# Three edits to a two-block fp32 network on one core: where tiles start, which PSUM banks GLA's scores use, how a layer norm gets its statistics

## The chip, the cores and the metric

The kernel runs on one core of one Trainium2 chip. TensorE multiplies matrices out of SBUF into PSUM, VectorE, ScalarE and GpSimd work on vectors, SyncE issues most DMAs. The metric is the device time of one execution in microseconds (us); smaller is better. The profile comes from one profiled execution.

## The reference

The input is a sequence of 256 rows of width 1024. A first block adds a hybrid mixer (three kinds of attention, gated and merged) and a convolutional FFN, both with RMS norms that are modulated by a vector. The second block has two layers: a gated linear attention (GLA, 4 heads of 128 keys and 256 values) and a dilated sliding-window attention (SWA), each followed by a layer norm. The part that the change touches:

```python
def layer_norm(x, g, b):
    mu = jnp.mean(x32, axis=-1, keepdims=True)
    xc = x32 - mu
    var = jnp.mean(xc * xc, axis=-1, keepdims=True)
    return (xc * lax.rsqrt(var + LN_EPS) * g + b)
...
def second_block(x, ...):
    for layer in range(DEPTH_2):
        y = gla_mixer(...) if layer == 0 else dilated_mixer(...)
        x = layer_norm(DEEPNORM_ALPHA * x + y, ln_g[layer], ln_b[layer])
...
# in gla_mixer: o = q S with a state S that decays by exp(log_a) at every row and key:
att = jnp.einsum('bhid,bhjd,bhijd->bhij', qc, kc, decay)
```

All weights, activations and results are float32.

## The kernel before

**Products in three parts.** An fp32 product is made of three fp32r matmuls: every operand is split into a high half and the rest, a low half, and `mm3` adds low stationary by high moving, high by low, and high by high in one PSUM bank. Weights are streamed by `Stream`: `_chunk` (L147 on) issues a DMA into `raw`, ScalarE copies it to `whi` (L158) and VectorE subtracts to get `wlo` (L159). Activations have tiles that end in `hi` and `lo` (`hhi`, `hlo`, `mhi`, `mlo`, `h2`, `x2`, `x3`, `fhi`/`flo`, `ohi`/`olo`, `shi`/`slo`).

**Two kinds of product.** In `wstat` (keys in1, inc, zg, br, up, gla, gk, kvk, sq) a 128x128 block of weights stands in TensorE and 256 columns of activations move. In `tokmm` (keys out, dn, gvg, gout, kvv, sout) 128 rows of the sequence stand and 512 columns of weights move. `wpair` can run a pair "fresh": first all high-activation products of eight blocks, then all low ones.

**Where tiles start.** `PAST` is 48 elements, 192 bytes: every low tile is allocated a little wider and used from 192 bytes past its start, whichever operand it is. The eight-block activations come from `big8`, with one tag for high tiles and one for low.

**GLA's scores.** The decayed scores of a half batch of 128 rows are built by levels. `gla_x` makes, for each of four heads, a bank `pm` with two matmuls (names glamr, Ll, Lh), its exponential E on ScalarE (L1024) and the products Xk, Xq on VectorE (L1027, L1028). `gla_p` then makes for each level four 128x64 matmuls (names Xq, Xk) into a bank, and VectorE copies from it under a mask into attT (COPY_PREDICATED, L1044, L1050). PSUM banks come from three rotating tags: `acc` (4), `mm` (2), `at` (2). `pm` and the score banks are all `at`. A scheduler with priorities puts these in between the products of GLA's v and g weights (names whi, wlo, x2hi, x2lo into acc); each engine then runs its instructions in that order.

**GLA's layer norm.** `layer_norm` walks a list of steps, `ORD3` for this one and `ORD4` for the last one. A step has a letter, a batch half (b = 0 or 1) and a column half. u: u = alpha x + y with a running sum; c: mean from the sums, then ScalarE's square of 1024 columns with a running sum (`junk`); w: (u − mean) times the gain; r: `rstd`, VectorE's add (`ms`) and GpSimd's power (`rs`, L364); n: scaling on ScalarE, N: on VectorE. TensorE then transposes the result x (L891), and the products of SWA need those transposes. A `Queue` keeps the steps of an engine in the written order. Helpers record many operations under line L193, so names tell them apart.

Of the kernel before, what the change touches and what calls it, by code (L numbers as in the profile page):

```python
# [8 lines left out]
F32 = mybir.dt.float32  # L9
F32R = mybir.dt.float32r  # L10
# [8 lines left out]
S = 256  # L19
# [8 lines left out]
SIDE = [("inc", 0)] + [("zg", i) for i in range(10)] + [("out", 0)] + [("up", i) for i in (3, 7, 11, 15)]  # L28
ORD1 = "s00 m01 s01 m00 r0 a00 S00 a01 S01 m10 s10 R0 A00 A01 s11 r1 m11 n00 n01 a10 S10 a11 S11 A10 R1 A11 N10 n11"
ORD2 = "s00 m01 s01 m00 r0 a00 a01 s10 m10 s11 r1 m11 a10 a11"  # L30
ORD3 = "u00 u01 c0 w00 w01 r0 n00 n01 u10 u11 c1 w10 w11 r1 N10 N11"
ORD4 = "u00 u01 c0 w00 w01 r0 u10 o00 u11 c1 o01 w10 r1 w11 o10 o11"
SC_SWA = float(128.0 ** -0.5)


PAST = 48

COLS = {}
# [64 lines left out]
class Stream:  # L103
# [31 lines left out]
    def _chunk(self, i):  # L135
        nc = self.nc
        key, ap, n, part = self.items[i]
        if part < 0:
            raw = self.early.tile([128, n], F32, tag="early", name="early", bufs=3)
        else:  # L140
            raw = self._raw()
        if not part:
            for o in range(0, n, 1024):
                nc.sync.dma_start(raw[:, o:o + 1024], ap[:, o:o + 1024])
            self.done.append(raw)
            return
        nc.sync.dma_start(raw[:, :n], ap)  # L147
        parts = []
        for o in range(0, n, part) if part > 0 else range(0, -part, 1024):
            m = min(part, n - o) if part > 0 else min(1024, -part - o)  # L150
            hi = self.pool.tile([128, 1024], F32R, tag="whi", name="whi", bufs=self.hlbufs)
            lo = self.pool.tile([128, 1088], F32R, tag="wlo", name="wlo", bufs=self.hlbufs)
            lo = lo[:, PAST:PAST + 1024]
            with ExitStack() as st:
                for ins in self.behind:
                    st.enter_context(self.tc.issue_after(ins))
                st.enter_context(self.tc.high_priority(self.pri))
                i0 = nc.scalar.activation(hi[:, :m], raw[:, o:o + m], AF.Copy)  # L158
                i1 = nc.vector.tensor_sub(lo[:, :m], raw[:, o:o + m], hi[:, :m].bitcast(F32))  # L159
                self.last = (i0.ins, i1.ins)  # L160
            parts.append((hi, lo))
        self.done.append((part, parts) if part > 0 else (raw, (1024, parts)))
# [68 lines left out]
def hybrid_blocks(ctx, tc, A, out, dbg=None):  # L231
# [22 lines left out]
    def at_t():  # L254
        return ps.tile([128, 512], F32, tag="at", name="at", bufs=2)
# [139 lines left out]
            mm(pr[:, 256 + b:257 + b], ssq[:, b * 128:(b + 1) * 128], ones[:, 0:1], h == 0 and b == 0, h == 3, True)  # L395

    def big8(dt, name, past=0):
        t = cn.tile([128, KK * S + 64 * (past > 0)], dt, name=name, tag="big8l" if past else "big8h")
        return t[:, past:past + KK * S].rearrange("p (k s) -> p k s", k=KK)

    hT = (big8(F32R, "hhi"), big8(F32R, "hlo", PAST))
# [375 lines left out]
    for i in range(2):  # L777
# [12 lines left out]
            branch2(0)  # L790
            branch2(1)
        gates(9 + 2 * i)
    mT = (big8(F32R, "mhi"), big8(F32R, "mlo", PAST))
    for i in range(4):
        if i > 1:
            branch2(i)
# [138 lines left out]
    def ffn_up(f):  # L935
        p = wpair(("up", f), h2, f == 0)
        u = wk.tile([128, S], F32, name="u", tag="u", bufs=2)
        cw = lambda i: col("cw", i * NF + f)
        act.activation(u, p[:, 0:S], AF.Identity, scale=cw(2), bias=col("cb", f))
        dve.scalar_tensor_tensor(u[:, 1:S], p[:, 0:S - 1], cw(1), u[:, 1:S], op0=OP.mult, op1=OP.add)  # L940
        dve.scalar_tensor_tensor(u[:, 2:S], p[:, 0:S - 2], cw(0), u[:, 2:S], op0=OP.mult, op1=OP.add)
        act.activation(u, u, AF.Gelu_apprx_tanh)
        a = wk.tile([128, S], F32, name="fa", tag="fa", bufs=2)
        dve.tensor_mul(a, u, p[:, S:2 * S])
        hi = wk.tile([128, 1, S], F32R, name="fhi", tag="fhi", bufs=6)
        lo = wk.tile([128, 1, S + 64], F32R, name="flo", tag="flo", bufs=6)[:, :, PAST:PAST + S]
        ins = act.activation(hi[:, 0, :], a, AF.Copy)
        ins2 = dve.tensor_sub(lo[:, 0, :], a, hi[:, 0, :].bitcast(F32))
        fact[f] = (hi, lo)
        return ins, ins2  # L950
# [13 lines left out]
    x2 = res.tile([128, 2, D], F32, name="x2")  # L964
    rms_residual(y2, x1, mod[3], x2, ORD2)
    dump("x2", x2)
    x2T = (big8(F32R, "x2hi"), big8(F32R, "x2lo", PAST))
    ws.behind = transposes(x2, ev_split(x2T), last_mm)


# [41 lines left out]
    def gla_x(b, u):  # L1012

        Xk = p3.tile([128, 4, 4, 128], F32, name="Xk", tag="Xk", bufs=1)
        Xq = p3.tile([128, 4, 4, 128], F32, name="Xq", tag="Xq", bufs=1)
        XK[b, u] = (Xk, Xq)
        nk, nq = (4, 4) if u == 0 else (3, 3) if b == 0 else (3, 4)
        for h in range(4):
            pm = at_t()
            r = glam[:, 4 * u * (1 + b):4 * u * (1 + b) + 4, :]  # L1020
            mm(pm, Ll[:, b, h * 128:(h + 1) * 128], r, True, False)
            mm(pm, Lh[:, b, h * 128:(h + 1) * 128], r, False, True)
            E = p3.tile([128, 4, 128], F32, name="E", tag="E", bufs=2)
            act.activation(E, pm, AF.Exp, scale=1.0 / 16.0)  # L1024
            bs = slice(b * 128, (b + 1) * 128)
            bc = lambda x, n: x[:, h, bs][:, None, :].to_broadcast([128, n, 128])
            dve.tensor_mul(Xk[:, h, 0:nk, :], E[:, 0:nk, :], bc(kT, nk))  # L1027
            dve.tensor_mul(Xq[:, h, 0:nq, :], E[:, 0:nq, :], bc(qT, nq))  # L1028
            if u and b == 0:
                dve.tensor_mul(keep[:, h, :], E[:, 3, :], kT[:, h, bs])  # L1030
            if h % 2:
                yield

    def gla_p(b, u):

        Xk, Xq = XK[b, u]
        for l in range(4):
            pp = at_t()
            if 4 * u + l < 7:
                n = 64 >> (4 * u + l)  # L1040
                late = lambda x: x.rearrange("p (g t s) -> p g t s", t=2, s=n)[:, :, 1, :]
                for h in range(4):
                    mm(pp[:, h * 64:(h + 1) * 64].rearrange("p (g s) -> p g s", s=n), Xk[:, h, l, :], late(Xq[:, h, l, :]), True, True)
                dve.copy_predicated(attT[:, 2 * b].rearrange("p h (g t s) -> p h g t s", t=2, s=n)[:, :, :, 1, :],  # L1044
                                    late(glamask[:, 4 * u + l, :])[:, None].to_broadcast([128, 4, 64 // n, n]),
                                    pp[:, 0:256].rearrange("p (h g s) -> p h g s", h=4, s=n))
                continue
            for h in range(4):
                mm(pp[:, h * 128:(h + 1) * 128], kT[:, h, b * 128:(b + 1) * 128], qT[:, h, b * 128:(b + 1) * 128], True, True)
            dve.copy_predicated(attT[:, 2 * b], glamask[:, 4 * u + l, :][:, None, :].to_broadcast([128, 4, 128]),  # L1050
                                pp.rearrange("p (h q) -> p h q", h=4))
        if u and b:
            pp = at_t()
            for h in range(4):
# [51 lines left out]
    for i in range(2, 4):  # L1106
        w = ws.get(("gvg", 4 + i), 1)
        work += [(x2T, 2 * i + u, w, u * 1024) for u in range(2)]
    gla_out(0)
    oT = (p3.tile([128, KK, S], F32R, name="ohi", tag="Xk"),  # L1110
          p3.tile([128, KK * S + 64], F32R, name="olo", tag="Xq")[:, PAST:PAST + KK * S].rearrange("p (k s) -> p k s", k=KK))
    pe = Queue(tc, pe, ws.last[0])

    def gated(b, u, last):
# [43 lines left out]
    def layer_norm(x, y, grow, brow, dst, utile, order, after=None):  # L1158


        qa, qd = Queue(tc, act, ws.last[0]), Queue(tc, dve, ws.last[1])
        su, r, u, w = {}, {}, {}, {}
        with tc.high_priority(BOOST):
            for step in order.split():
                op, b, h = step[0], int(step[1]), int(step[2:] or 0)
                c = half(h)
                if op == "u":
                    if not h:
                        su[b] = cn.tile([128, 6], F32, name="su", tag="su", bufs=2)
                        u[b], w[b] = utile(b), utile(b + 2)  # L1170
                    qd.scalar_tensor_tensor(u[b][:, c], x[:, b, c], ALPHA, y[b][h], op0=OP.mult, op1=OP.add, accum_out=su[b][:, h:h + 1])
                elif op == "c":
                    qd.tensor_scalar(su[b][:, 2:3], su[b][:, 0:1], su[b][:, 1:2], -1.0 / (32.0 * D), op0=OP.add, op1=OP.mult)
                    qd.tensor_scalar(su[b][:, 3:4], su[b][:, 2:3], -32.0, None, op0=OP.mult)
                    qa.activation(junk(), u[b], AF.Square, bias=su[b][:, 2:3], scale=1.0 / 32.0, accum_out=su[b][:, 4:5])
                elif op == "w":
                    qd.scalar_tensor_tensor(w[b][:, c], u[b][:, c], su[b][:, 3:4], grow[:, c], op0=OP.subtract, op1=OP.mult)
                elif op == "r":
                    r[b] = rstd(su[b][:, 4:5], 1, 1e-5, qd)
                elif op == "n":  # L1180
                    qa.activation(dst[:, b, c], w[b][:, c], AF.Copy, scale=r[b][:, 0:1])
                elif op == "N":
# [106 lines left out]
    def swa_pv(i, parts=(slice(0, S),)):  # L1289
# [1 line left out]
        kv, pT = i // 2, pTs[i]  # L1291
        v = lambda g, b: sl(sv, ALL, b, slice((2 * g + kv) * 128, (2 * g + kv + 1) * 128))
        hi = wk.tile([128, 2, S], F32R, name="shi", tag="shi", bufs=2)
        lo = wk.tile([128, 2 * S + 64], F32R, name="slo", tag="slo", bufs=2)[:, PAST:PAST + 2 * S].rearrange("p (u s) -> p u s", u=2)
        for u in range(2):
            sact[2 * i + u] = sl((hi, lo), ALL, slice(u, u + 1))
        for qs in parts:
# [148 lines left out]
```

## Time and profile before

| what | value |
|---|---|
| median of 3 runs | 735.49 us (733.15 to 735.66) |
| profiled execution, its own time | 735.57 us |
| its span, first to last instruction | 733.6 us |
| mean granted TensorE clock | 0.987 |
| instructions | 12191 |

The span is what the trace covers; some 2 us lie around it. In the trace, PE is TensorE's matmuls and PEld its weight loads, DVE is VectorE, ACT ScalarE, POOL GpSimd. A matmul's shown length overlaps that of the next, so its cost is taken from start to start. `[1.22 <-ACT E L1024]` behind a row means that the engine was idle 1.22 us ahead of it and that ScalarE's instruction on E ended the wait.

### The profile page before, as it was taken

What the parts mean: (1) busy time and instruction counts of PE and PEld (TensorE: products, weight loads), DVE (VectorE), ACT (ScalarE), POOL (GpSimd) and SP (SyncE); (2) the same over time, 40 slices, a digit from 0 to 9 for tenths busy, and PEclk for the clock granted to TensorE, in tenths of its full rate; (3) what the DMA queues carried; (4) which work ended last, traced back from release to release, by engine and by line L of the source; (5) the groups of instructions that cost most, each with busy time, mean ns of one, the idle gap of its engine ahead of it and who ended that gap; (6) DMA issues with size and microseconds to landing.
All of it is one profiled execution on the core that took longest, in us unless ns stands there. A gap on an engine that the chain in (4) does not pass through costs nothing. (4 is left out here: it accounts for less than half of the span.)

```text
span 733.6 us, 12191 instructions
## 1 busy us (share of the span) xinstructions
PE 703.0 (96%) x4878; PEld 637.2 (87%) x4878; DVE 546.9 (75%) x933; ACT 406.9 (55%) x675; POOL 20.1 (3%) x34
## 2 busy tenths in 40 slices
PE   5999999999989999999999899999989999999995
PEld 4888888998869999998999797888879999999984
DVE  5877969898967776768666766675778689777866
ACT  4447788546547545554544685344546566565542
POOL 0001000000010000000000200001000000000000
PEclk9999999999998999999999999999999999999998
DMA  8996767567744675658645364331347755433201
GB/s 322 422 354 222 281 258 292 207 245 261 242 164 171 236 259 197 230 193 309 245 172 202 125 240 174 116 115 58 144 186 248 255 195 193 156 132 136 96 1 57
DMA packets 24600, 148.74 MB, mean 203 GB/s; under 512 B 2992, under 2 KB 3248, under 8 KB 9568
## 3 DMA queue, kind: packets, MB, share of 16 engines
q1 hardware_dynamic: 21888, 139.05, 51.8%
q0 software_dynamic: 1280, 5.18, 2.2%
q10 hardware_dynamic: 1376, 3.74, 1.5%
q8 instruction: 38, 0.62, 0.3%
q14 instruction: 18, 0.15, 0.1%
HBM read 145.86 MB, written 2.10 MB: 202 GB/s over the span
## 5 line engine op out<-in xcount | busy, mean ns | idle before, releaser
L159 DVE TENSOR_TENSOR wlo<-raw,whi 128x1024 fp32r<-128x1024 f32 (+1 forms) x193 | 231.3, 1210 | 65.6 <-ACT whi L158 65.1
L158 ACT ACTIVATE whi<-raw 128x1024 fp32r<-128x1024 f32 (+1 forms) x193 | 199.3, 1050 | 97.2 <-PE acc L262 42.6
L262 PE MATMUL mm<-h2hi,wlo 128*128 128x256 f32 x352 | 98.6, 281 | 0.0
L262 PE MATMUL mm<-h2hi,whi 128*128 128x256 f32 x352 | 98.5, 281 | 0.0
L262 PE MATMUL mm<-h2lo,whi 128*128 128x256 f32 x352 | 97.3, 283 | 0.0
L262 PE MATMUL mm<-x3hi,wlo 128*128 128x256 f32 x304 | 85.6, 283 | 0.0
L262 PE MATMUL mm<-x3hi,whi 128*128 128x256 f32 x304 | 84.6, 280 | 0.0
L262 PE MATMUL mm<-x3lo,whi 128*128 128x256 f32 x304 | 83.4, 282 | 0.0
L262 PEld LDWEIGHTS mm<-h2hi,wlo 128*128 128x128 f32 x352 | 67.2, 191 | 0.4
L262 PEld LDWEIGHTS mm<-h2hi,whi 128*128 128x128 f32 x352 | 67.2, 191 | 0.0
L262 PEld LDWEIGHTS mm<-h2lo,whi 128*128 128x128 f32 x352 | 65.4, 189 | 0.4
L262 PE MATMUL mm<-hhi,wlo 128*128 128x256 f32 x208 | 60.0, 289 | 0.7 <-DVE wlo L159 0.4
L262 PE MATMUL mm<-hlo,whi 128*128 128x256 f32 x208 | 59.9, 288 | 0.0
L262 PE MATMUL mm<-hhi,whi 128*128 128x256 f32 x208 | 59.3, 285 | 0.0
L262 PEld LDWEIGHTS mm<-x3hi,wlo 128*128 128x128 f32 x304 | 57.6, 190 | 0.0
L262 PEld LDWEIGHTS mm<-x3hi,whi 128*128 128x128 f32 x304 | 57.5, 189 | 0.0
L262 PEld LDWEIGHTS mm<-x3lo,whi 128*128 128x128 f32 x304 | 56.1, 188 | 0.0
L262 PEld LDWEIGHTS mm<-hhi,wlo 128*128 128x128 f32 x208 | 39.8, 191 | 2.8 <-PE mm L262 1.0
L262 PEld LDWEIGHTS mm<-hlo,whi 128*128 128x128 f32 x208 | 39.8, 191 | 0.8 <-issue 0.8
L262 PEld LDWEIGHTS mm<-hhi,whi 128*128 128x128 f32 x208 | 39.7, 191 | 0.6 <-issue 0.5
L445 DVE SCALAR_TENSOR_TENSOR adacc<-raw,cact,adacc 128x1024 f32<-128x1024 f32 x28 | 35.7, 1275 | 0.2
L262 PE MATMUL acc<-whi,flo 128*128 128x512 f32 x88 | 34.9, 397 | 0.0
(355 smaller groups left out, 1608.4 us busy)
## 6 DMA issues: line engine op xcount, KB each, us to landing
raw<-in_w_up_dram SPq DMA_DIRECT2D x22, 1024.0 KB, 4.7
raw<-in_w_ada_dram SPq DMA_DIRECT2D x16, 1024.0 KB, 4.9
raw<-in_swa_q_dram SPq DMA_DIRECT2D x16, 1024.0 KB, 5.2
raw<-in_w_zg_dram SPq DMA_DIRECT2D x12, 1024.0 KB, 5.6
raw<-in_w_dn_dram SPq DMA_DIRECT2D x11, 1024.0 KB, 4.8
raw<-in_w_ada_dram SPq DMA_DIRECT2D x16, 512.0 KB, 9.0
early<-in_w_in_dram SPq DMA_DIRECT2D x8, 1024.0 KB, 7.7
raw<-in_gla_vg_dram SPq DMA_DIRECT2D x8, 1024.0 KB, 4.9
```

The lines of the kernel that those rows point to most:

```text
L158: i0 = nc.scalar.activation(hi[:, :m], raw[:, o:o + m], AF.Copy)
L159: i1 = nc.vector.tensor_sub(lo[:, :m], raw[:, o:o + m], hi[:, :m].bitcast(F32))
L262: return pe.matmul(o, l, r, start=start, stop=stop, skip_group_check=share)
L445: dve.scalar_tensor_tensor(a, w, c, a, op0=OP.mult, op1=OP.add)
```

## The change

1. A list `STILL` names the keys whose weights stand. `wlo` is used from 192 bytes past only for those; for weights that move, it starts where its tile starts. The low halves of activations that stand (mlo, flo, olo, slo) and x2lo also lose the 192 bytes; hlo, h2lo and x3lo keep them. `big8` has one tag with two buffers, every tile 64 elements wider.
2. In `gla_x` every second head's `pm` is an mm bank. In `gla_p` two levels share a bank, one bank is `at` and one `mm`, all matmuls of a group are written ahead of its masked copies, and the diagonal has an `at` bank of its own.
3. In GLA's layer norm the sum and ScalarE's square are replaced by VectorE's BN_STATS on each column half and one BN_AGGR; r stands right behind c; ScalarE scales three of the four pieces instead of two. The last layer norm keeps its operations under new letters (U, q). The small tile is `lns` [128, 16] in place of `su` [128, 6].

```diff
-ORD3 = "u00 u01 c0 w00 w01 r0 n00 n01 u10 u11 c1 w10 w11 r1 N10 N11"
+ORD3 = "u00 v00 u01 v01 c0 r0 w00 w01 n00 n01 u10 v10 u11 v11 c1 r1 w10 n10 w11 N11"
+STILL = ("in1", "inc", "zg", "br", "up", "gla", "gk", "kvk", "sq")
...
-            lo = lo[:, PAST:PAST + 1024]
+            lo = lo[:, PAST:PAST + 1024] if key[0] in STILL else lo[:, 0:1024]
...
-        t = cn.tile([128, KK * S + 64 * (past > 0)], dt, name=name, tag="big8l" if past else "big8h")
+        t = cn.tile([128, KK * S + 64], dt, name=name, tag="big8r", bufs=2)
...
-    mT = (big8(F32R, "mhi"), big8(F32R, "mlo", PAST))
+    mT = (big8(F32R, "mhi"), big8(F32R, "mlo"))
...
-        lo = wk.tile([128, 1, S + 64], F32R, name="flo", tag="flo", bufs=6)[:, :, PAST:PAST + S]
+        lo = wk.tile([128, 1, S], F32R, name="flo", tag="flo", bufs=6)
...
-    x2T = (big8(F32R, "x2hi"), big8(F32R, "x2lo", PAST))
+    x2T = (big8(F32R, "x2hi"), big8(F32R, "x2lo"))
...
-            pm = at_t()
+            pm = mm_t() if h % 2 else at_t()
...
+        levels = [l for l in range(4) if 4 * u + l < 7]
+        banks = [mm_t() if i else at_t() for i in range(2)]
+        for l in levels:
+            n = 64 >> (4 * u + l)
             for h in range(4):
+                o = banks[l // 2][:, l % 2 * 256 + h * 64:l % 2 * 256 + (h + 1) * 64]
+                mm(o.rearrange("p (g s) -> p g s", s=n), Xk[:, h, l, :], late(Xq[:, h, l, :], n), True, True)
...
-        su, r, u, w = {}, {}, {}, {}
+        st, r, u, w = {}, {}, {}, {}
...
+                        st[b] = cn.tile([128, 16], F32, name="lns", tag="lns", bufs=2)
...
+                elif op == "v":
+                    qd.bn_stats(st[b][:, 6 * h:6 * h + 6], u[b][:, c])
                 elif op == "c":
...
+                    qd.bn_aggr(st[b][:, 12:14], st[b][:, 0:12])
```

TensorE's order where the first group of GLA's scores begins, before:

```order
L262 MATMUL acc<-whi,x2hi 128x512
L262 MATMUL at<-glamr,Ll 128x512
L262 MATMUL at<-glamr,Lh 128x512
L262 MATMUL at<-glamr,Ll 128x512
L262 MATMUL at<-glamr,Lh 128x512
L262 MATMUL acc<-whi,x2lo 128x512
L262 MATMUL acc<-wlo,x2hi 128x512
L262 MATMUL acc<-whi,x2hi 128x512
L262 MATMUL acc<-whi,x2lo 128x512
L262 MATMUL at<-glamr,Ll 128x512
L262 MATMUL at<-glamr,Lh 128x512
```

The same place with the change:

```order
L264 MATMUL acc<-whi,x2hi 128x512
L264 MATMUL at<-glamr,Ll 128x512
L264 MATMUL at<-glamr,Lh 128x512
L264 MATMUL mm<-glamr,Ll 128x512
L264 MATMUL mm<-glamr,Lh 128x512
L264 MATMUL at<-glamr,Ll 128x512
L264 MATMUL at<-glamr,Lh 128x512
L264 MATMUL mm<-glamr,Ll 128x512
L264 MATMUL mm<-glamr,Lh 128x512
L264 MATMUL acc<-whi,x2lo 128x512
```

The four heads' pairs now stand together, alternating between the two tags. Some 30 instructions further on TensorE comes to the first score blocks; before:

```order
L262 MATMUL acc<-whi,x2hi 128x512
L262 MATMUL at<-Xq,Xk 128x64 x6
L262 MATMUL acc<-whi,x2lo 128x512
L262 MATMUL acc<-wlo,x2hi 128x512
L262 MATMUL at<-Xq,Xk 128x64 x2
L262 MATMUL acc<-whi,x2hi 128x512
```

The same place with the change:

```order
L264 MATMUL acc<-whi,x2hi 128x512
L264 MATMUL at<-Xq,Xk 128x64 x3
L264 MATMUL mm<-Xq,Xk 128x64 x3
L264 MATMUL at<-glamr,Ll 128x512
L264 MATMUL at<-glamr,Lh 128x512
L264 MATMUL at<-Xq,Xk 128x64 x5
L264 MATMUL mm<-Xq,Xk 128x64 x5
L264 MATMUL mm<-glamr,Ll 128x512
```

Six blocks (three heads) still stand ahead of the fourth head's, which now all follow one pair of the next group. VectorE's order in GLA's layer norm, before:

```order
L193 SCALAR_TENSOR_TENSOR lnu,su<-x_4397,acc 128x512 x2
L193 TENSOR_SCALAR su<-su 128x1 x2
L193 SCALAR_TENSOR_TENSOR lnw<-lnu,su,r_lng_5525 128x512 x2
L193 TENSOR_SCALAR ms<-su 128x1
L193 TENSOR_SCALAR x_5522<-lnw,rs 128x512 x2
```

The same with the change (the second batch half):

```order
L195 SCALAR_TENSOR_TENSOR lnu<-x_4397,acc 128x512
L195 BN_STATS lns<-lnu 128x6
L195 SCALAR_TENSOR_TENSOR lnu<-x_4397,acc 128x512
L195 BN_STATS lns<-lnu 128x6
L195 BN_AGGR lns<-lns 128x2
L195 TENSOR_SCALAR ms<-lns 128x1
L195 SCALAR_TENSOR_TENSOR lnw<-lnu,lns,r_lng_5519 128x512 x2
L195 TENSOR_SCALAR x_5516<-lnw,rs 128x512
```

The two small sums became BN_STATS and BN_AGGR, `ms` moved ahead of `lnw`, and one of the two scalings of x left VectorE for ScalarE. GpSimd's and SyncE's orders are the same in both.

## Rows read from the trace of the kernel before

**Rows 1.** The page: busy time of each engine, its share of the span, its instructions.

```profile
PE 703.0 (96%) x4878; PEld 637.2 (87%) x4878; DVE 546.9 (75%) x933; ACT 406.9 (55%) x675; POOL 20.1 (3%) x34
```

**Rows 2.** Windows: stretch, length; busy (instructions) per engine, granted clock, DMA share, GB/s.

```profile
10.00:50.00 40.00, 36.05 (x214) 28.97 (x214) 33.21 (x67) 15.38 (x24) 0.72 (x1) 1.00 1.01 405
530.00:547.00 17.00, 14.20 (x66) 11.67 (x65) 10.44 (x24) 7.42 (x13) 1.10 (x2) 0.92 0.49 184
545.00:547.50 2.50, 2.50 (x13) 2.50 (x12) 1.25 (x5) 2.09 (x6) 0.00 (x0) 0.50 0.48 167
547.00:700.00 153.00, 152.91 (x1201) 147.60 (x1200) 122.12 (x212) 92.44 (x145) 1.13 (x2) 1.00 0.50 176
```

**Rows 3.** Chain that ended last, from 546 us: start, length, what, how many instructions.

```profile
546.65 17.21 PE mm L262 x144
...
635.27 5.57 PE acc L262 x24
```

**Rows 4.** Timeline of TensorE from 548 us: start, length, line, operation, count.

```profile
548.85 1.10 PE L262 MATMUL mm<-x3lo,whi 128*128 128x256 f32 x8
549.78 0.28 PE L262 MATMUL mm<-x3hi,wlo 128*128 128x256 f32 x1
...
551.67 1.10 PE L262 MATMUL mm<-x3lo,whi 128*128 128x256 f32 x8
```

**Rows 5.** Timeline of TensorE from 624 us: the first of six, and what follows them.

```profile
624.68 0.40 PE L262 MATMUL at<-pTh,svl 128*128 128x512 f32 x1
...
626.07 0.28 PE L262 MATMUL at<-pTh,svl 128*128 128x256 f32 x1
```

**Rows 6.** Timeline of all engines, 448 to 459 us.

```profile
448.95 0.39 PE L262 MATMUL acc<-whi,x2lo 128*128 128x512 f32 x1
...
449.91 1.09 ACT L1024 ACTIVATE E<-at 128x512 f32<-128x512 f32 x2
...
450.56 0.50 PE L262 MATMUL at<-glamr,Ll 128*128 128x512 f32 x1 [1.22 <-ACT E L1024]
...
456.27 1.45 PE L262 MATMUL at<-Xq,Xk 128*128 128x64 f32 x12
...
456.54 0.68 DVE L1028 TENSOR_TENSOR Xq<-E,gqT 128x512 f32<-128x512 f32 x1
...
457.53 0.48 PE L262 MATMUL acc<-whi,x2lo 128*128 128x512 f32 x1
...
457.85 0.39 PE L262 MATMUL acc<-wlo,x2hi 128*128 128x512 f32 x1
458.08 0.55 PE L262 MATMUL at<-Xq,Xk 128*128 128x64 f32 x4
```

**Rows 7.** Timeline of all engines, 540 to 546 us.

```profile
540.83 0.69 DVE L193 SCALAR_TENSOR_TENSOR lnu<-x,acc 128x512 f32<-128x512 f32 x1 [2.07 <-PE acc L262]
...
541.56 0.40 DVE L193 TENSOR_SCALAR su<-su 128x1 f32<-128x1 f32 x2
...
541.87 1.15 ACT L193 ACTIVATE junk<-lnu,su 128x1024 bf16<-128x1024 f32 x1 [1.94 <-DVE su L193]
542.00 1.41 DVE L193 SCALAR_TENSOR_TENSOR lnw<-lnu,su,r_lng 128x512 f32<-128x512 f32 x2
...
543.33 0.15 DVE L193 TENSOR_SCALAR ms<-su 128x1 f32<-128x1 f32 x1
...
543.55 0.55 POOL L364 TENSOR_TENSOR rs<-ms,mhalf 128x1 f32<-128x1 f32 x1 [4.99 <-DVE ms L193]
544.14 0.88 DVE L193 TENSOR_SCALAR x<-lnw,rs 128x512 f32<-128x512 f32 x2 [0.67 <-POOL rs L364]
544.68 1.97 PE L891 MATMUL acc<-ident,x 128*128 128x128 f32 x8 [2.67 <-DVE x L193]
```

**Rows 8.** Groups of VectorE by form: line, what, count, busy us, mean ns, idle before.

```profile
L1271 DVE TENSOR_SCALAR sP<-sP,sst 128x512 f32<-128x512 f32 x16 | 7.7, 486 | 0.4
...
L393 DVE TENSOR_REDUCE ssq<-sq 128x256 f32<-128x512 f32 x4 | 2.8, 695 | 3.2 <-ACT sq L391 3.1
```

More of the change, by code (lines that the diff above doesn't have):

```diff
@@ L30 @@
 ORD2 = "s00 m01 s01 m00 r0 a00 a01 s10 m10 s11 r1 m11 a10 a11"
-ORD3 = "u00 u01 c0 w00 w01 r0 n00 n01 u10 u11 c1 w10 w11 r1 N10 N11"
-ORD4 = "u00 u01 c0 w00 w01 r0 u10 o00 u11 c1 o01 w10 r1 w11 o10 o11"
+ORD3 = "u00 v00 u01 v01 c0 r0 w00 w01 n00 n01 u10 v10 u11 v11 c1 r1 w10 n10 w11 N11"
+ORD4 = "U00 U01 q0 w00 w01 r0 U10 o00 U11 q1 o01 w10 r1 w11 o10 o11"
 SC_SWA = float(128.0 ** -0.5)
+STILL = ("in1", "inc", "zg", "br", "up", "gla", "gk", "kvk", "sq")
 PAST = 48
@@ L1036, in gla_p @@
         Xk, Xq = XK[b, u]
[L1037 to L1047, printed above, removed]
-            for h in range(4):
-                mm(pp[:, h * 128:(h + 1) * 128], kT[:, h, b * 128:(b + 1) * 128], qT[:, h, b * 128:(b + 1) * 128], True, True)
-            dve.copy_predicated(attT[:, 2 * b], glamask[:, 4 * u + l, :][:, None, :].to_broadcast([128, 4, 128]),
-                                pp.rearrange("p (h q) -> p h q", h=4))
+        late = lambda x, n: x.rearrange("p (g t s) -> p g t s", t=2, s=n)[:, :, 1, :]
@@ new lines, in gla_p @@
+        levels = [l for l in range(4) if 4 * u + l < 7]
+        banks = [mm_t() if i else at_t() for i in range(2)]
+        for l in levels:
+            n = 64 >> (4 * u + l)
+            for h in range(4):
+                o = banks[l // 2][:, l % 2 * 256 + h * 64:l % 2 * 256 + (h + 1) * 64]
+                mm(o.rearrange("p (g s) -> p g s", s=n), Xk[:, h, l, :], late(Xq[:, h, l, :], n), True, True)
+        if u:
+            pd = at_t()
+            for h in range(4):
+                mm(pd[:, h * 128:(h + 1) * 128], kT[:, h, b * 128:(b + 1) * 128], qT[:, h, b * 128:(b + 1) * 128], True, True)
@@ new lines, in gla_p @@
+        for l in levels:
+            n = 64 >> (4 * u + l)
+            dve.copy_predicated(attT[:, 2 * b].rearrange("p h (g t s) -> p h g t s", t=2, s=n)[:, :, :, 1, :],
+                                late(glamask[:, 4 * u + l, :], n)[:, None].to_broadcast([128, 4, 64 // n, n]),
+                                banks[l // 2][:, l % 2 * 256:l % 2 * 256 + 256].rearrange("p (h g s) -> p h g s", h=4, s=n))
+        if u:
+            dve.copy_predicated(attT[:, 2 * b], glamask[:, 7, :][:, None, :].to_broadcast([128, 4, 128]),
+                                pd.rearrange("p (h q) -> p h q", h=4))
@@ L1109, in hybrid_blocks @@
     gla_out(0)
-    oT = (p3.tile([128, KK, S], F32R, name="ohi", tag="Xk"),
-          p3.tile([128, KK * S + 64], F32R, name="olo", tag="Xq")[:, PAST:PAST + KK * S].rearrange("p (k s) -> p k s", k=KK))
+    oT = tuple(p3.tile([128, KK, S], F32R, name=n, tag=t) for n, t in (("ohi", "Xk"), ("olo", "Xq")))
     pe = Queue(tc, pe, ws.last[0])
@@ L1166, in layer_norm @@
                 c = half(h)
-                if op == "u":
+                if op in "uU":
                     if not h:
-                        su[b] = cn.tile([128, 6], F32, name="su", tag="su", bufs=2)
+                        st[b] = cn.tile([128, 16], F32, name="lns", tag="lns", bufs=2)
                         u[b], w[b] = utile(b), utile(b + 2)
-                    qd.scalar_tensor_tensor(u[b][:, c], x[:, b, c], ALPHA, y[b][h], op0=OP.mult, op1=OP.add, accum_out=su[b][:, h:h + 1])
+                    sums = dict(accum_out=st[b][:, h:h + 1]) if op == "U" else {}
+                    qd.scalar_tensor_tensor(u[b][:, c], x[:, b, c], ALPHA, y[b][h], op0=OP.mult, op1=OP.add, **sums)
+                elif op == "q":
+                    qd.tensor_scalar(st[b][:, 2:3], st[b][:, 0:1], st[b][:, 1:2], -1.0 / (32.0 * D), op0=OP.add, op1=OP.mult)
+                    qd.tensor_scalar(st[b][:, 12:13], st[b][:, 2:3], -32.0, None, op0=OP.mult)
+                    qa.activation(junk(), u[b], AF.Square, bias=st[b][:, 2:3], scale=1.0 / 32.0, accum_out=st[b][:, 13:14])
+                elif op == "v":
+                    qd.bn_stats(st[b][:, 6 * h:6 * h + 6], u[b][:, c])
                 elif op == "c":
-                    qd.tensor_scalar(su[b][:, 2:3], su[b][:, 0:1], su[b][:, 1:2], -1.0 / (32.0 * D), op0=OP.add, op1=OP.mult)
-                    qd.tensor_scalar(su[b][:, 3:4], su[b][:, 2:3], -32.0, None, op0=OP.mult)
-                    qa.activation(junk(), u[b], AF.Square, bias=su[b][:, 2:3], scale=1.0 / 32.0, accum_out=su[b][:, 4:5])
+                    qd.bn_aggr(st[b][:, 12:14], st[b][:, 0:12])
                 elif op == "w":
-                    qd.scalar_tensor_tensor(w[b][:, c], u[b][:, c], su[b][:, 3:4], grow[:, c], op0=OP.subtract, op1=OP.mult)
+                    qd.scalar_tensor_tensor(w[b][:, c], u[b][:, c], st[b][:, 12:13], grow[:, c], op0=OP.subtract, op1=OP.mult)
                 elif op == "r":
-                    r[b] = rstd(su[b][:, 4:5], 1, 1e-5, qd)
+                    r[b] = rstd(st[b][:, 13:14], 1, 1e-5, qd)
                 elif op == "n":
@@ L1293, in swa_pv @@
         hi = wk.tile([128, 2, S], F32R, name="shi", tag="shi", bufs=2)
-        lo = wk.tile([128, 2 * S + 64], F32R, name="slo", tag="slo", bufs=2)[:, PAST:PAST + 2 * S].rearrange("p (u s) -> p u s", u=2)
+        lo = wk.tile([128, 2, S], F32R, name="slo", tag="slo", bufs=2)
         for u in range(2):
```

## The prediction

> **What bounds the kernel now.** I read the shares of busy time first: TensorE's matmuls are busy for 703.0 us of a span of 733.6 [rows 1]. The windows say the same by stretch: over 547 to 700 us TensorE is busy 152.91 us of 153.00 at full clock, over 530 to 547 only 14.20 of 17.00, and over 10 to 50 us 36.05 of 40.00, with the DMA engines at a share of 1.01 [rows 2]. So there are two ways to gain: make a matmul start sooner after the one before it, or take out one of the few waits. The chain of waits gives the first in numbers. A run of 144 matmuls of 256 columns takes 17.21 us with its first few at half clock, and one of 24 of 512 columns takes 5.57 us, 232 ns each [rows 3]. For 256 columns at full clock the timeline has stretches of one kind: 8 matmuls that move x3lo take 549.78 − 548.85 = 0.93 us, 116 ns each; 16 that move x3hi take 551.67 − 549.78 = 1.89 us, 118 ns each [rows 4].
>
> **Part A, placement.** No instruction goes or comes; the question is only the start-to-start time. In the kernel before, the low halves lie 192 bytes past and the high halves do not. The change puts low and high at one offset in all products where activations stand (out, dn, gvg, gout, kvv, sout: 264 triples, 792 matmuls of 512 columns, counted from the code's loops) and keeps the 192 bytes where weights stand (1080 triples of 256 columns), except that the moving x2lo loses it (72 triples). One group before already has all its tiles at one offset: pTh and pTl against svh and svl. Its six matmuls of 512 columns take 626.07 − 624.68 = 1.39 us, 232 ns each [rows 5], the same as the 232 of the mixed kind [rows 3]. I take that: 0 for the 792. For x2T the nearest rows are those of one kind, (2 × 118 + 116) / 3 = 117.3 ns, against 17.21 us less its slow start, about 116: 216 × 1.5 = +0.3 us. Bounds: the two kinds of rows 4 differ by 2 ns at 256 columns, so I allow twice that, 4 to 5 ns, at 512, either way: 792 × 4.8 = ±3.8 us.
>
> [...]
>
> **Part B, the scores of GLA.** The timeline at 449 us shows the wait [rows 6]: the third head's first matmul (glamr, Ll) starts at 450.56 after 1.22 us idle, released by ScalarE's exponential E at 449.91, since both `at` banks were full; the matmul before began at 448.95 and its successor would have followed 0.23 later, so 1.4 us are lost. After the change the four heads have four banks and the wait goes. What is late next is Xq of the fourth head: written from 456.54, 0.68 long, so ready at 457.22, and read by the Xq,Xk block that starts at 458.08. With 1.4 us less ahead of it TensorE comes there at 456.68 and waits 0.54 if VectorE comes no earlier (its weight copies stand in between). So 0.85 come through. Second, a matmul of 512 columns behind a 64-column block loses something: 457.53 to 457.85 is 0.32 us [rows 6] where 0.23 is usual. By the instruction order the blocks fall from 16 to 11: 5 × 0.09 = 0.45. The copies under the mask stay the same 16 in number, only behind all matmuls of their group. Sum −1.3 us. Bounds: both gains whole and a few waits of 0.1 to 0.3 for `at` banks gone too, −2.3; new waits, since the mm banks are now also held until VectorE's masked copies and ScalarE's exponentials, two of about 0.5 us net of the gain, +1.0.
>
> **Part C, GLA's layer norm.** The timeline at 540 us [rows 7] is a chain without cover: once TensorE's last product is done, lnu (540.83, 0.69), two small sums (541.56, 0.40), ScalarE's square (541.87, 1.15, and its read-out), ms (543.33), POOL's power (543.55, 0.55), x (544.14), and TensorE's transposes begin at 544.68 after 2.67 us idle. VectorE's lnw (542.00, 1.41) lies beside the square. Only the second batch half (b = 1) shows; the first lies under TensorE's products. In its place: lnu to 541.52, BN_STATS of the second half, BN_AGGR, ms, the power. BN_STATS does not occur before. Nearest is the reduction of VectorE over 512 elements, 695 ns; below it a plain 512-element operation with 486 ns; above it two passes of the reduction, 1.4 us [rows 8]. I take 0.69, as it reads and reduces the same number of elements. BN_AGGR, on 12 numbers, I put at one of the small sums, 0.2. That gives 542.2, 542.4, ms to 542.6, the power from 542.65 to 543.2; lnw's first half runs beside it (0.7, to 543.3), and then ScalarE multiplies the first half of x, which costs there about what E costs for the same size (1.09 for two, [rows 6]), to 543.9. TensorE resumes at 544.0 instead of 544.68: −0.7 us. Bounds: at 0.486, −0.9. At 1.4 the chain is back where it was, 0. [...]
>
> **Sum.** A +0.3, B −1.3, C −0.7: −1.7 us on the profiled execution's own time of 735.57, so 733.9. The runs shown have a median of 735.49, which is the same. The second layer norm keeps its instructions, and what it may change lies in the tail.
>
> **Rivals.**
> 1. Like offsets do help at 512 columns. Price: −3.8 by the bound of A, so about 730. For it: two kinds of rows at 256 columns differ [rows 4], so offsets do something. Against: rows 5.
> 2. Slower: what counts is not the offset between low and high but where the moving operand starts. The allocation of the changed kernel puts the large tiles 128 bytes further, because the small-tile pool has grown by 128 bytes (the new `lns` tile beside `su`'s tag): the moving weights and standing activations stand at 128 past a multiple of 256, not on it, and the change then does not do what it says. If that costs each matmul the 2 ns by which rows 4 differ, and double at 512 columns, the price is 3240 × 2 + 792 × 4 = 9.6 us: 743. It decides the sign from 0.4 ns a matmul (1.7 us over 4032). For it: the tiles do move. Against: x3lo, moved from 192 past, runs at 116 ns and x3hi, from a multiple, at 118 [rows 4].
> 3. The gains don't come through: the wait for Xq eats B, and BN_STATS takes twice the reduction: 735 to 736.5. For it: VectorE's order puts a weight's low half ahead of that Xq; against: TensorE is the only engine that is nearly full there.
> 4. The first 50 us run at a DMA share of 1.01 [rows 2]; if the transfers slow down because their tiles moved, TensorE starts its stretches later. Rows give no price other than that 1% of those 40 us is 0.4 us; I allow up to 1: 734.9. [...]
>
> **How the numbers follow.** Chances: the forecast 0.50, rival 1 0.20, rival 2 0.13, rival 3 0.12, rival 4 0.05. The forecast's own range is 731.5 to 736 (C and B at their bounds, A within 1). About 0.5%, 3.7 us, is what a measurement of this kernel can tell from no change: 731.8 to 739.2 count as the same. Faster: rival 1 and a fifth of the forecast, 0.30. Slower: most of rival 2 and a little of the rest, 0.15. Same: 0.55. The range reaches from 728.5, which holds most of rival 1, to 741, which holds the milder half of rival 2.
>
> **What would show it.** A: matmuls of 512 columns in the out, dn and gout stretches still 232 ns apart (228 would be rival 1, 236 rival 2), and those of 256 columns still 116 (118 and more: rival 2). B: no idle time before the third head's glamr pair, a wait of about 0.5 us before the Xq,Xk block of the fourth head, and the stretch 447 to 530 us shorter by 1.3. C: BN_STATS near 0.69 us, TensorE resuming 3.2 us after that lnu starts instead of 3.85, and still half clock for about 2.5 us. The prediction is wrong if the start-to-start times move by more than 1 ns, since 4032 matmuls multiply it.

## The result and the profile after

The changed kernel takes 731.02 us in the median of 12 runs (728.44 to 733.43), the kernel before 734.63 in the median of 12 (731.63 to 737.73). The ratio is 0.9939, 95% interval 0.9923 to 0.9956: 4.5 us faster, between 3.2 and 5.7. The profiled execution took 728.44 us, the shortest of the 12, so its trace shows more gain than the median does.

The page of the changed kernel, its row of busy times:

```profile
PE 696.4 (96%) x4878; PEld 634.1 (87%) x4878; DVE 549.2 (76%) x930; ACT 404.7 (56%) x672; POOL 21.1 (3%) x34
```

TensorE has the same 4878 matmuls as in [rows 1], busy 6.6 us less. The windows of the changed kernel (columns as in [rows 2]; the layer norm now lies some 6.5 us earlier):

```profile
10.00:50.00 40.00, 35.26 (x214) 28.21 (x214) 32.94 (x67) 15.96 (x26) 0.72 (x1) 0.87 1.01 403
...
538.00:541.00 3.00, 2.92 (x19) 2.44 (x19) 1.69 (x5) 2.47 (x8) 0.00 (x0) 1.00 0.68 265
```

The start is no faster: the DMA share of 10 to 50 us is 1.01 as before. Behind the layer norm (538 to 541 us) the granted clock is 1.00, where [rows 2] had 0.50. The chain that ended last, from the same places as [rows 3] and one more:

```profile
539.17 17.83 PE mm L264 x144
...
598.59 5.58 PE mm L264 x48
...
628.37 5.47 PE acc L264 x24
```

A run of 48 matmuls of 256 columns takes 5.58 us, 116 ns each, as in the stretches of [rows 4]. The 24 of 512 columns take 5.47 us where [rows 3] has 5.57: 228 ns instead of 232. The down-projection shows it over a longer stretch, since 264 matmuls of 512 columns lie in it between others. The summaries of two tiles give first and last start; of the kernel before:

```profile
L262 PE MATMUL acc<-whi,flo x88: 389/389/794, 241.3 to 409.0; 128*128 128x512 f32 x88
L262 PE MATMUL acc<-whi,fhi x88: 393/397/398, 241.8 to 409.4; 128*128 128x512 f32 x88
```

and of the changed kernel:

```profile
L264 PE MATMUL acc<-whi,flo x88: 387/389/799, 238.3 to 405.0; 128*128 128x512 f32 x88
L264 PE MATMUL acc<-whi,fhi x88: 388/389/400, 238.8 to 405.4; 128*128 128x512 f32 x88
```

409.4 − 241.3 = 168.1 us became 405.4 − 238.3 = 167.1: 1.0 us over 264 matmuls, 3.8 ns each.

The stretch ahead of it is 3.0 us shorter as well (241.3 to 238.3 us), and the change explains little of that: of the products that got like offsets only out lies there, 96 matmuls or some 0.4 us. The trace of the kernel before has a granted clock of 0.52 from 131.0 to 134.5 us, with 18 matmuls in it, and this one 1.00, with 31. In the experiments below the down-projection begins at 239.0 us with placement alone and at 238.5 on multiples of 256, and at 242.9 with GLA's part alone, which has the placement of before. What the rest of the 3.0 us comes from, these traces do not show.

The group of pTh and pTl, on which the prediction built [rows 5], has not moved at all. Its timeline in the changed kernel:

```profile
617.77 0.40 PE L264 MATMUL at<-pTh,svl 128*128 128x512 f32 x1
...
619.15 0.28 PE L264 MATMUL at<-pTh,svl 128*128 128x256 f32 x1
```

1.38 us for six, against 1.39.

In GLA the wait of [rows 6] is gone. The timeline of the changed kernel:

```profile
445.16 0.39 PE L264 MATMUL mm<-glamr,Ll 128*128 128x512 f32 x1
...
446.38 0.60 ACT L1026 ACTIVATE E<-at 128x512 f32<-128x512 f32 x1
...
452.37 0.68 DVE L1030 TENSOR_TENSOR Xq<-E,gqT 128x512 f32<-128x512 f32 x1
...
452.62 0.40 PE L264 MATMUL at<-glamr,Lh 128*128 128x512 f32 x1
...
453.11 1.33 PE L264 MATMUL at<-Xq,Xk 128*128 128x64 f32 x10
```

The fourth head's pair begins at 445.16, so all four pairs run before ScalarE's first E at 446.38. The next wait, for the fourth head's Xq (ready at 452.37 + 0.68 = 453.05), holds TensorE until 453.11; the pair before began at 452.62, so some 0.25 us are lost there. In the list of TensorE's waits (total us, times, longest) the kernel before has two lines of GLA's scores,

```profile
PE at L262 <- ACT E L1024: 1.2, 1, 1.2
...
PE at L262 <- DVE attT L1044: 0.3, 1, 0.3
```

and neither has a counterpart in the list of the changed kernel.

The layer norm, beside [rows 7]; the timeline of the changed kernel:

```profile
534.35 0.69 DVE L195 SCALAR_TENSOR_TENSOR lnu<-x,acc 128x512 f32<-128x512 f32 x1 [0.31 <-PE acc L264]
535.07 0.69 DVE L195 BATCH_NORM_STATS2 lns<-lnu 128x6 f32<-128x512 f32 x1
535.80 0.21 DVE L195 BATCH_NORM_AGGREGATE lns<-lns 128x2 f32<-128x12 f32 x1
...
536.12 1.40 DVE L195 SCALAR_TENSOR_TENSOR lnw<-lnu,lns,r_lng 128x512 f32<-128x512 f32 x2
536.28 0.99 POOL L366 TENSOR_TENSOR rs<-ms,mhalf 128x1 f32<-128x1 f32 x1 [3.82 <-DVE ms L195]
537.30 0.72 ACT L195 ACTIVATE x<-lnw,rs 128x512 f32<-128x512 f32 x1 [3.47 <-POOL rs L366]
...
538.08 1.09 PE L893 MATMUL acc<-ident,x 128*128 128x128 f32 x8 [2.55 <-ACT x L195]
```

BN_STATS takes 0.69 us and BN_AGGR 0.21, as forecast. But GpSimd's power, 0.55 us in [rows 7], takes 0.99, with VectorE's lnw running beside it. The transposes begin 538.08 − 534.35 = 3.73 us after lnu, where [rows 7] has 3.85: 0.12 us came of the 0.65 forecast. They then take 1.09 us instead of 1.97, at full clock.

### The profile page after: what moved, and what is told of

Its sections match the earlier page's. It is cut to its first block, busy times and chain, and to the rows that moved or that the text cites. A ratio compares the mean times of both kernels' runs of the same rounds, so it can differ in the third digit from the quotient of the medians.

```text
span 726.4 us, 12187 instructions
## 1 busy us (share of the span) xinstructions
PE 696.4 (96%) x4878; PEld 634.1 (87%) x4878; DVE 549.2 (76%) x930; ACT 404.7 (56%) x672; POOL 21.1 (3%) x34
```

## The experiments

**Each part alone.** Three kernels start from the one before and take one part of the change each.

The first has the lines on STILL, big8 and the low halves:

```diff
-            lo = lo[:, PAST:PAST + 1024]
+            lo = lo[:, PAST:PAST + 1024] if key[0] in STILL else lo[:, 0:1024]
...
-    mT = (big8(F32R, "mhi"), big8(F32R, "mlo", PAST))
+    mT = (big8(F32R, "mhi"), big8(F32R, "mlo"))
```

The second has `gla_x` and `gla_p` of the change:

```diff
-            pm = at_t()
+            pm = mm_t() if h % 2 else at_t()
...
+        banks = [mm_t() if i else at_t() for i in range(2)]
```

The third has `ORD3` and `layer_norm` of the change:

```diff
-ORD3 = "u00 u01 c0 w00 w01 r0 n00 n01 u10 u11 c1 w10 w11 r1 N10 N11"
+ORD3 = "u00 v00 u01 v01 c0 r0 w00 w01 n00 n01 u10 v10 u11 v11 c1 r1 w10 n10 w11 N11"
```

> The kernel before with part A alone: low and high halves at one offset where activations stand. Its large tiles stand on multiples of 256 bytes. Theory (what counts is the offset of the operands against each other): the 512-column matmuls of the out, dn, gvg, gout and sout products go from 232 ns to about 228 as in the changed kernel, the x2 matmuls of 256 columns lose 2 ns, in all -2.1 us, about -0.3% (ratio 0.997). Rival (where the moving operand starts counts, and the changed kernel is at 128): here the rows differ from those of the changed kernel by 2 ns or more, and the total by 4 us or more either way. My forecast as recorded had this part at +0.3 us.

> The kernel before with part B alone: heads' pm and score levels over at and mm banks. Theory: the 1.4 us wait ahead of the third head's glamr pair goes, five changes from 64 to 512 columns fewer, small waits gone: the stretch from the first glamr to the first gout product shorter by 2.0 us (ratio 0.997). Rival (the recorded bound): a wait for the fourth head's Xq takes back half, -0.9 us. Second rival: mm banks held longer cost as much as is gained, 0.

> The kernel before with part C alone: BN_STATS and BN_AGGR in GLA's layer norm. It also moves the large tiles by 128 bytes, low halves still 192 bytes past everywhere. Theory: -0.7 us between the last gout product and the first x3 product, nothing elsewhere (ratio 0.999). Rival (the start of tiles counts): the start-to-start times of 512 and 256 columns move by 2 ns or more, at least 6 us either way.

Placement alone: ratio 0.9953 (0.9934 to 0.9972), −3.5 us. The chain has the same 5.47 us for the 24 matmuls of 512 columns:

```profile
631.99 5.47 PE acc L263 x24
```

GLA alone: 0.9971 (0.9954 to 0.9987), −2.1 us. Summaries of the first glamr and the first gout product, in the kernel before:

```profile
L262 PE MATMUL at<-glamr,Ll x16: 388/395/501, 447.3 to 494.6; 128*128 128x512 f32 x16
...
L193 PE MATMUL acc<-whi,olo x8: 389/402/478, 517.4 to 523.2; 128*128 128x512 f32 x8
```

and with GLA's part alone:

```profile
L262 PE MATMUL at<-glamr,Ll x8: 389/395/476, 448.8 to 494.0; 128*128 128x512 f32 x8
...
L193 PE MATMUL acc<-whi,olo x8: 389/402/478, 516.7 to 522.5; 128*128 128x512 f32 x8
```

From 447.3 to 517.4 are 70.1 us, from 448.8 to 516.7 67.9: −2.2 us, so neither rival's bill came.

The layer norm alone: 1.001 (0.9988 to 1.0032), nothing that can be measured. The power is slow here too, and the lower clock comes after the transposes, over the products of x3. Its timeline and one window:

```profile
540.68 0.99 POOL L364 TENSOR_TENSOR rs<-ms,mhalf 128x1 f32<-128x1 f32 x1 [3.94 <-DVE ms L193]
...
542.48 1.09 PE L891 MATMUL acc<-ident,x 128*128 128x128 f32 x8 [2.54 <-ACT x L193]
```

```profile
544.00:547.00 3.00, 3.00 (x15) 3.00 (x15) 3.00 (x9) 3.00 (x8) 0.00 (x0) 0.50 0.98 376
```

This kernel's large tiles stand 128 bytes further than before, with the 192 bytes kept, and nothing got slower by it that these runs can tell.

**On multiples of 256.** The changed kernel's own tiles are 128 bytes past a multiple of 256. This one packs three small tiles under one tag, which takes the 128 bytes back:

```diff
-    bad1 = cn.tile([128, 16], F32, name="bad1")
+    bad1 = cn.tile([128, 16], F32, name="bad1", tag="lns", bufs=2)
...
-    wis = cn.tile([128, 2, 4], F32, name="wis", tag="bad1")
+    wis = cn.tile([128, 2, 4], F32, name="wis", tag="lns", bufs=2)
...
-    cumq = cn.tile([128, 2, 4], F32, name="cumq", tag="su", bufs=2)
+    cumq = cn.tile([128, 2, 4], F32, name="cumq", tag="lns", bufs=2)
```

> The changed kernel with its small tiles packed so that the large tiles stand on multiples of 256 bytes (three small tiles share one tag). Theory (only offsets against each other count): the same time as the changed kernel within 1 us, -4.5 us against before, 512 columns at 227 to 228 ns. Rival (where tiles start counts): 2 ns a matmul more or less, 8 us either way against the changed kernel; -2 us or better would mean that the change as made gave away part of its gain.

0.9943 (0.9923 to 0.9962), beside 0.9939 of the change. The chain has both kinds as the change has them:

```profile
628.36 5.47 PE acc L264 x24
...
672.66 5.58 PE mm L264 x48
```

Rival 2 of the prediction falls: whether a tile stands on a multiple of 256 or 128 past one is worth nothing that these runs can tell.

**Like offsets everywhere, and other distances.** The changed kernel with PAST = 0, and the kernel before with PAST = 32 (128 bytes):

```diff
-PAST = 48
+PAST = 0
```

> The changed kernel with the 192 bytes taken away everywhere, so that low and high halves are at one offset where weights stand too. Theory (like offsets help at 512 moving columns and hurt at 256, as the x2 products showed: 117.8 ns after, 115.7 before): the 1008 triples of 256 columns that still had the 192 bytes go from 115.7 to 117.8 ns a matmul, 3024 x 2.1 = +6.3 us against the changed kernel, so about +1.8 us against before (ratio 1.002); the 512-column products stay at 227 to 228. Rival (like offsets are better at every size, the x2 products have another reason): 256 columns at 115 or less, faster than the changed kernel.

> The kernel before with low halves 128 bytes past instead of 192, everywhere. Theory (a matmul whose moving operand and the next standing one start at unlike places loses, whatever the distance): 512 columns at 231 to 232 ns as before, 256 columns at 115 to 116, time as before within 1.5 us. Rival (128 bytes count as like): 512 columns at 227 to 228 and 256 columns at 117.8, so +6.8 - 2.6 = about +4 us.

Like offsets everywhere: 1.0086 (1.0056 to 1.0116), 10.8 us slower than the change (1.0086 − 0.9939, times 734.6). 128 bytes: 1.0072 (1.0046 to 1.0099), 5.3 us slower than before. The chain with like offsets everywhere:

```profile
604.64 5.76 PE mm L264 x48
...
641.76 5.47 PE acc L264 x24
```

and with 128 bytes in place of 192:

```profile
608.64 5.66 PE mm L262 x48
...
638.75 5.60 PE acc L262 x24
```

Like offsets give 5.76 / 48 = 120 ns at 256 columns (116 with 192 bytes), and keep 228 at 512. At 256 columns 4 ns times the 3024 matmuls that changed is 12 us, about what the run shows. I had put it at half of that, from the x2 products, of which only some are alike. 128 bytes give 118 ns and 233: unlike offsets lose at 512 columns at both distances, and at 256 the distance counts. So neither of my two theories was whole.

Like offsets do not give 228 ns to every product of 512 columns. In kvv, rows of x3 stand, and in the kernel with like offsets everywhere all its operands have one offset. Its triples of 512 columns alternate with triples of 256; from the start of one of 512 to the triple behind it:

```profile
568.64 0.40 PE L264 MATMUL acc<-whi,x3lo 128*128 128x512 f32 x1
...
569.34 0.28 PE L264 MATMUL acc<-whi,x3lo 128*128 128x256 f32 x1
```

That is 0.70 us for three. Over all 16 such triples the starts are 232.3 ns apart here, 230.1 in the change, where x3lo keeps its 192 bytes, and 230.5 in the kernel before. With pTh and pTl above this makes two groups of 512 columns that run at 232 with like offsets.

Two more distances, from the changed kernel (PAST = 16 and PAST = 56, 64 and 224 bytes, where weights stand):

> The changed kernel with low halves 64 bytes past instead of 192 where weights stand. Theory (distances count by their place in 256 bytes, and 64 is 192 the other way round): 256 columns at 115 to 116 ns, time as with the change, ratio 0.993 to 0.995. Rival (192 itself is the good distance; every step nearer to 0 comes nearer to the 120 ns of like offsets): 117 to 120 ns, 4 to 13 us slower than the change.

> The changed kernel with low halves 224 bytes past instead of 192 where weights stand, 32 bytes short of the next 256. Theory (distance in 256 bytes): between like offsets at 120 ns and 192 at 115.7, so about 118, 6 to 7 us slower than the change, ratio about 1.003. Rival (any unlike place does as well as 192): 115 to 116 ns and the time of the change.

64 bytes: 1.0017 (0.9996 to 1.0038). 224 bytes: 1.0006 (0.9985 to 1.0026). Both give back the whole gain, 5 to 6 us against the change. The chain with 64 bytes, and behind it that with 224:

```profile
638.47 5.65 PE mm L264 x48
```

```profile
643.43 5.66 PE mm L264 x48
```

118 ns both. Of 0, 64, 128, 192 and 224 bytes, 192 is the best where weights stand; 64 is not 192 the other way round, so the theory of the first of these runs is wrong, and its rival's 117 to 120 ns came. The theory of the second had its 118 ns right and its time 1 to 2 us too long.

**The power by itself.** The changed kernel with lnw ahead of ms in the second batch half:

```diff
-ORD3 = "u00 v00 u01 v01 c0 r0 w00 w01 n00 n01 u10 v10 u11 v11 c1 r1 w10 n10 w11 N11"
+ORD3 = "u00 v00 u01 v01 c0 r0 w00 w01 n00 n01 u10 v10 u11 v11 c1 w10 w11 r1 n10 N11"
```

> The changed kernel with lnw ahead of ms and the power in the second batch half, so that GpSimd's power runs with VectorE idle. Theory (the power was held up by VectorE's lnw, which reads two tiles of SBUF): the power takes 0.55 us in place of 0.99; the start of the transposes is later by 1.4 - 0.44 = about 0.9 us against the lnu of that half, 4.6 us instead of 3.7. Rival (BN_AGGR's output or the tile's place makes the power slow): it stays at 0.99, and the start is 1.4 us later, at 5.1.

The timeline:

```profile
537.30 0.69 DVE L195 SCALAR_TENSOR_TENSOR lnu<-x,acc 128x512 f32<-128x512 f32 x1 [0.32 <-PE acc L264]
...
540.55 0.55 POOL L366 TENSOR_TENSOR rs<-ms,mhalf 128x1 f32<-128x1 f32 x1 [5.14 <-DVE ms L195]
...
541.68 1.10 PE L893 MATMUL acc<-ident,x 128*128 128x128 f32 x8 [3.20 <-DVE x L195]
```

With VectorE idle the power takes 0.55 us again. The transposes begin 541.68 − 537.30 = 4.38 us after lnu, 0.65 later than in the change and far from the rival's 5.1. The ratio is 0.9971 (0.9944 to 0.9998), 2.4 us slower than the change by the middle values, with intervals that overlap. The trace of the kernel before had the same pair of cases, in the first block's norm:

```profile
214.60 1.28 DVE L193 TENSOR_TENSOR xr<-x,grow 128x512 f32<-128x512 f32 x2
214.76 0.92 POOL L840 TENSOR_TENSOR rs<-ms,mhalf 128x1 f32<-128x1 f32 x1 [2.67 <-DVE ms L193]
...
216.17 0.68 DVE L193 TENSOR_TENSOR x<-acc,grow 128x512 f32<-128x512 f32 x1
216.33 0.54 POOL L840 TENSOR_TENSOR rs<-ms,mhalf 128x1 f32<-128x1 f32 x1 [0.65 <-DVE ms L193]
```

Behind a VectorE operation with two tiles in SBUF (xr: x, grow) the power takes 0.92 us, beside one with a tile in PSUM (acc) 0.54. lnw reads two tiles in SBUF as well (lnu, r_lng). In the change the power begins 0.16 us after lnw's first half, which is 0.74 us long and ends at 536.12 + 0.74 = 536.86, and it ends 0.41 us after that, at 537.27. By what lnw holds it up, no run shows. The rows do not show lnw's second half held up by the power in turn: the two halves take 1.40 us, as the 1.41 of [rows 7].

**The change without its layer norm.**

Parts 1 and 2 as in the change, `ORD3` and `layer_norm` as before:

```diff
-ORD3 = "u00 v00 u01 v01 c0 r0 w00 w01 n00 n01 u10 v10 u11 v11 c1 r1 w10 n10 w11 N11"
+ORD3 = "u00 u01 c0 w00 w01 r0 n00 n01 u10 u11 c1 w10 w11 r1 N10 N11"
```

> The changed kernel with the layer norm of before (sum and ScalarE's square), so parts A and B alone. Theory (part C gives about nothing, since the power behind lnw takes 0.99 us in place of 0.55): the ratio to before stays at 0.993 to 0.995, as with the change. Rival (C is worth its recorded 0.7 us or more): slower than the changed kernel by 0.7 us or more, ratio 0.995 to 0.996.

0.9951 (0.9929 to 0.9974). That is 0.9 us slower than the change by the middle values, with intervals that overlap: theory and rival are not told apart, and the layer norm's part is too small for these runs.

## Why the prediction was right or wrong

The sign is right and the time lies in the stated range, but 731.0 against 733.9 is a gain 2.6 times the forecast (4.5 us for 1.7). It lies outside the forecast's own 731.5 to 736, in the part that the range held for rival 1; and by the prediction's own sign of being wrong, start-to-start times that move by more than 1 ns, the step on part A was wrong. Two terms were too small and one too large.

**Part A failed at the step "I take that: 0 for the 792".** The group of rows 5 was taken to stand for like offsets. It has like offsets, and takes 232 ns before and after; something else holds it there. Of the 792 matmuls, the 48 of kvv did not get like offsets, since x3lo keeps its 192 bytes; the prediction counted them in. The other 744 went from 232 to 228: 3.8 ns each by the down-projection's stretch, 744 × 3.8 = −2.8 us. This is rival 1 at the number it named (228), with four fifths of its bound of 4.8 ns. The x2 products lost 0.5 us (the prediction had 0.3): before they run from 413.4 to 441.7, after from 409.4 to 438.2, as these summaries of tiles show.

```profile
L262 PE MATMUL mm<-x2hi,wlo x72: 276/277/387, 413.4 to 441.4; 128*128 128x256 f32 x72
L262 PE MATMUL mm<-x2hi,whi x72: 276/278/384, 414.4 to 441.7; 128*128 128x256 f32 x72
```

```profile
L264 PE MATMUL mm<-x2hi,wlo x72: 274/280/386, 409.4 to 438.0; 128*128 128x256 f32 x72
L264 PE MATMUL mm<-x2hi,whi x72: 277/279/384, 410.4 to 438.2; 128*128 128x256 f32 x72
```

So A is −2.3 us by the rows, and −3.5 (−4.8 to −2.1) by the run of this part alone. The rows to look at were in the trace of the kernel before: in the 88 triples of the down-projection the median time from start to next start is 227, 230 and 236 ns for the three matmuls, in the order of `mm3`, and 227 for each of them in the changed kernel. So one of the three already ran at what all three could reach.

**Part B had the mechanism right and its terms wrong in size.** The wait went, and the wait for Xq took its place, with 0.25 us instead of 0.54 (0.1 with GLA's part alone), since E and Xq came earlier too. The 0.45 for fewer changes between 64 and 512 columns was mostly not there to be had. In the kernel before, behind the block of 4 that starts at 458.08 [rows 6]:

```profile
458.44 0.48 PE L262 MATMUL acc<-whi,x2hi 128*128 128x512 f32 x1
...
460.17 1.89 PE L262 MATMUL at<-Xq,Xk 128*128 128x64 f32 x16
461.87 0.48 PE L262 MATMUL acc<-whi,x2lo 128*128 128x512 f32 x1
```

The block of 4 takes 458.44 − 458.08 = 0.36 us and the one of 16 takes 1.70, so the 12 more cost 1.34, 0.112 each. A block of 4 is then 0.09 us shorter than 4 × 0.112, and that pays for the 0.09 that the matmul behind it loses. The term that was too small is the sum of small waits, set at nothing in the middle value: at the wait for attT the next matmul starts 0.72 us after the one before it, 0.5 later than usual, and five more starts in this stretch are 0.03 to 0.11 late, 0.3 in all; with GLA's part alone these are gone. 1.4 + 0.5 + 0.3 less 0.1 for Xq is 2.1 us of the 2.2 measured, where 1.3 were forecast and the bound was 2.3.

**Part C had the instruction right and the neighbour wrong.** BN_STATS at 0.69 and BN_AGGR at 0.2 are as taken. The step that failed is "the power from 542.65 to 543.2; lnw's first half runs beside it": lnw does not run beside the power without cost, it holds it up by 0.44 us. The start of the transposes gained 0.12 us in place of 0.65. What differs beyond that is the granted clock. The forecast kept about 2.5 us at half clock. In the traces of the change and of the kernel on multiples of 256 the clock is 1.00 in every microsecond from 538 to 545 us, behind this layer norm; the transposes and the 144 matmuls behind them take 1.09 + 17.83 = 18.92 us in the change, where the kernel before has 1.97 + 17.21 = 19.18. In the trace of the layer norm alone the clock falls, later, to 0.50 from 544 to 547 us. With 64 bytes, with the same layer norm and the same idle time ahead of the transposes (2.54 us, 2.55 in the change), it is 0.58 from 540 to 541 us and 0.50 from 541 to 543, right over the transposes, which take 1.97 us again and not 1.09:

```profile
540.40 1.97 PE L893 MATMUL acc<-ident,x 128*128 128x128 f32 x8 [2.54 <-ACT x L195]
```

With 0 and 224 bytes, with the same layer norm too, the transposes and the 144 matmuls take 1.30 + 18.61 and 1.09 + 18.78 us, 1.0 more than in the change. 120 and 118 ns in place of 116 would be 0.6 and 0.3 of that; that the clock fell there as well is my estimate from the rest.

So the shorter wait did not by itself keep the clock up, and that it stayed up in the profiled execution of the change cannot be counted as part C's gain. With that, its part is not to be told from nothing.

**The sum.** −2.3 − 2.2 − 0.1 is −4.6 us against −4.5 (−5.7 to −3.2) measured. Rival 2 and rival 3 did not come. Nothing speaks for rival 4: the kernels at 0 and at 128 bytes past a multiple of 256 differ by 0.0004 in their ratios, and in their traces the down-projection begins at 238.5 and 238.3 us.

**Left open.** Why the pT group and kvv run at 232 ns with like offsets, when five other products of 512 columns run at 228; why 192 bytes is best at 256 columns; and what decides whether the clock falls behind the layer norm, where a wait of 2.55 us was followed by 1.00 in the change and one of 2.54 us by 0.50 with 64 bytes.

## What to carry to other kernels

In this kernel, where nearly every matmul has a standing operand of its own, where the operands start against each other is worth some 2 to 4% of a matmul (4 of 228 ns at 512 moving columns, 2 to 4 of 116 at 256), and the better choice depends on the product: like offsets in five products of 512 moving columns, nothing in two more, 192 bytes apart at 256. It has to be measured for each product by the start-to-start time, and a group of rows stands for another only if it also has its tiles and its order. And before two steps are put side by side on VectorE and GpSimd, look in the trace for a place where they already are. A clock that fell in one trace and not in another is no gain of the change until runs of one kernel agree on it.

## What the runs showed that was not expected

The offset alone moves a matmul of 256 columns from 116 to 120 ns, and one of 512, in five products, from 228 to 232 or 233, while moving all tiles by 128 bytes together changes neither (5.47 us for 24 and 5.58 for 48 at both places). GpSimd's power on 128 numbers takes 0.55 us alone and 0.92 to 0.99 behind a VectorE operation that reads two SBUF tiles.
